# A trunk with two PEER layers on one core: the first tile's x in PSUM, half of a low half on GpSimd, gates in smaller pieces, and another share of the gathers in u

## The chip, the core and the metric

The kernel runs on one core of one Trainium2 chip. The metric is the device time of one execution in microseconds (us). TensorE is PE in the profile, VectorE DVE, ScalarE ACT, GpSimd POOL; SP only issues transfers.

## What is computed

Two layers over 512 tokens of width 1024, each a mixer (chunked gated linear attention in the first, stick-breaking attention in the second, both with memory attention) followed by a PEER retrieval. The change lies in PEER alone:

```python
def peer(x, w_q, subkeys, u_tab, v_tab):
    q = (xf @ w_q).reshape(N, PEER_HEADS, 2, PEER_QHALF)
    s = jnp.einsum('nhpd,hpkd->nhpk', q, subkeys)
    top_s, top_i = lax.top_k(s, PEER_TOPK)
    ...
    idx = jnp.take_along_axis(cand_i, best_pos, axis=-1)
    g = jax.nn.softmax(best_s, axis=-1)
    def apply_experts(args):
        xt, it, gt = args
        act = jax.nn.gelu(jnp.einsum('nd,nhkd->nhk', xt, u_tab[it]), approximate=False)
        return jnp.einsum('nhk,nhkd->nd', gt * act, v_tab[it])
```

There are 16384 experts with a row of 1024 in each of the tables u and v. Each token takes 8 heads x 16 experts.

## The kernel before

Most tokens don't gather. For 352 of the 512 tokens the kernel multiplies x with the whole table u (128 blocks of 128 experts), applies gelu, multiplies with a dense matrix of gates that is zero but for the chosen experts, and multiplies the result with the whole table v (for 384 tokens). Products in fp32 are made of a high and a low half: `split` (L86) lets ScalarE round a block to the high half (uh), and VectorE subtracts it from the block to get the low half (ul). TensorE then makes three products per chunk: 24 matmuls for a block of u.

The first tile of 128 tokens gathers its expert rows instead: `gather` (L1165) is an indirect DMA, issued by GpSimd, of one row for each of the 128 tokens, 512 KB into one of four buffers `gr`. In u a VectorE instruction multiplies gr with the tile's x and sums it (a product); in v one adds gr times a weight to `va`. There are 128 of each, and 32 more gathers in u for the last 32 tokens (the side gathers, with their own x, `xr`). Three gathers are kept ahead (PF).

**Order.** The orders on PE, ACT, DVE and POOL are those in which the code is written (`manual_schedule`); SP's is made by the framework's scheduler. The u stage is a loop of `ublock(b)`, b = 0 to 128. A block does in this order: load block b+2 and make its uh (`prep`; the subtraction that makes ul is only put on a list, `later`); the 24 matmuls into `ph`; gelu of the block before; a step or two of building gates (`gst`: one-hots `ob` on VectorE, scaled ones `obl`, matmuls into `pg`, and from there the gates `gt`, written to DRAM as `Gd`); some selection work (`work`: top-16 of the scores and indices), in which `topk16` may hand the listed subtraction to GpSimd; then `flush` subtracts on VectorE what is still listed; then gather products, as many as `room` gives credit for (`gus`). `room` is a count of VectorE time from constants (BLK, SUM, LOW, HOT, REST), with lowest and highest values GU, GUA, GUX, GUZ, GUM; WB and WB0 are the credit of the selection.

Gates come in 24 groups of 16 tokens (`Gd[sub]`), the last two of them for the side gathers' tokens. Before, all of u uses a PSUM pool of eight banks.

In v a loop runs over 128 blocks, each with `vprep(b + 2)` (load vr, split it into vh and vl, multiply gates with the activations to w, split w), 18 matmuls into six accumulators, and gathers by the credit `vb` (L1844), which spreads what u has left. Gates are loaded by `preload` (L1790): those of a group of 16 blocks (GB) are 24 x 128 x 256 numbers and come in four pieces (GP) in four blocks, from ten blocks (GA) ahead. The first group of six blocks (g0, in a tile named keep) is loaded whole at block 126, where `vprep` begins (BX).

Of the kernel before, what the change touches and what calls it, by code (L numbers as in the profile page):

```python
# [10 lines left out]
F32 = mybir.dt.float32  # L11
# [3 lines left out]
AF = mybir.ActivationFunctionType  # L15
# [59 lines left out]
def psum(E, name="ps", tag="ps"):  # L75
    p, tags = E.ps
    return p.tile([P, 512], F32, tag=tag, name=name, bufs=tags[tag])

# [7 lines left out]
def split(E, raw, name, pool=None, tag="", later=None, eng=None, rows=None):  # L86

    nc = E.nc
    eng = eng or nc.vector
    pool = pool or E.hl  # L90
    if callable(pool):
        hi, lo = pool(f"{name}h"), pool(f"{name}l")
    else:
        hi = pool.tile([P, D], F32R, tag=tag + "hi", name=f"{name}h")
        lo = pool.tile([P, D], F32R, tag=tag + "lo", name=f"{name}l")
    if rows is None:
        nc.scalar.activation(hi, raw, AF.Copy)  # L97
        sub = lambda eng=eng: eng.tensor_sub(lo, raw, hi.bitcast(F32))  # L98
    else:
        nc.scalar.activation(hi, raw, AF.Copy, scale=rows)  # L100
        sub = lambda: eng.scalar_tensor_tensor(lo, raw, rows, hi.bitcast(F32), op0=ALU.mult, op1=ALU.subtract)
    if later is None:
        sub()
    else:
        later.append(sub)
    return hi, lo
# [888 lines left out]
def x_to_T(E, t, tag="ps"):  # L995

    nc = E.nc
    for g in range(2):
        ps = psum(E, name="xtp", tag=tag)
        for j in range(4):  # L1000
# [57 lines left out]
T0 = T - TD  # L1058
KEEP = 16
KB = P - KEEP  # L1060
TS = 16
# [8 lines left out]
GB = 16  # L1070
GA = 10
GP = 4
OT = 4
DT = 8
WB, WB0 = 820, 1600
GU, GUA, GUX, GUZ, GUM = 700, 1500, 1600, 1300, 2400
BG = 118
BLK, SUM, LOW, HOT, REST = 3950, 450, 1150, 1900, 1.12
WP = 1100
# [10 lines left out]
GR = 1.2  # L1090
BX = 126
GR2 = 1.5
# [23 lines left out]
def peer(E, mixer, wq, sk, ut, vt, un, lng, lnb, out_dram=None, follow=()):  # L1116
# [11 lines left out]
    with ExitStack() as pp:  # L1128
# [17 lines left out]
        next(mixer)  # L1146
        pp.enter_context(psum_pool(E, ps=8))
        for _ in mixer:
# [13 lines left out]

        gcount, known = [0], [0]

        def gather(tab, k, idx=None):  # L1165
# [35 lines left out]
        def gather_u():  # L1201
            nu, pend = 0, []

            def issue():
# [6 lines left out]
                if nu < min(P, known[0]):  # L1211
                    pend.append((gh, nu, E.x[:, 0], gather(un, nu)))
                    nu += 1
                    return True
# [6 lines left out]
            while pend:  # L1221
                dst, k, xr, gr = pend.pop(0)
                V.scalar_tensor_tensor(gr, gr, 1.0, xr, op0=ALU.mult, op1=ALU.mult, accum_out=dst[:, k:k + 1])
                if dst is not gh and k == TS - 1:
# [34 lines left out]
        with ExitStack() as up:  # L1259
# [3 lines left out]
            nc.scalar.dma_start(skt, sk)  # L1263
            later = []
            did = dict(low=0, hot=0, sum=0)

            def topk16(*jobs, pool=True):
# [15 lines left out]
                for v, i, s, s2 in jobs:  # L1283
                    nc.vector.max_index(i[:, 8:16], v[:, 8:16], s2)
                return WP if done else 0
# [433 lines left out]
            gst = Stream(gates(list(range(0, S0, OT))), gates(list(range(0, P, OT))), side_gates(0), gates(list(range(0, P, OT))), side_gates(1))  # L1719
            lead.c = -2000.0  # L1720
            ab, ph = None, None
            big = keep = g0 = None

            def ublock(b):
# [26 lines left out]
                else:  # L1751
                    work(WB if ready else WB0)
                flush()
                hot, low, sums = (did[k] - was[k] for k in ("hot", "low", "sum"))
                room = BLK + SUM * sums - HOT * hot - LOW * (1 - low) - REST * (lead.used + work.used - used)
                if b < P - 1:
                    gus(min(max(room, GU), GUA if work.q else GUX if b < BG else GUZ), GUM)
                if LOG:
                    print("block", b, len(work.q), len(gst.q), len(gus.q), gcount)
# [28 lines left out]
        pre = {}  # L1788

        def preload(i):  # L1790

            for c, c1 in zip(gcuts[1:], gcuts[2:]):
                q = i - max(1, c - GA)
                if 0 <= q < GP:
                    if q == 0:
                        pre[c] = new_gates(c, c1)
                    load_gates(pre[c], vorder[c], vorder[c] + c1 - c, slice(q * NSUB // GP, (q + 1) * NSUB // GP))

        def vprep(i):
# [5 lines left out]
            if i in gcuts:  # L1805
                if i == 0:
                    vp["g"] = g0
                    load_gates(g0, b, b + G0)
                else:
                    vp["g"] = pre.pop(i)  # L1810
                vp["i"] = i
# [26 lines left out]
        with written:  # L1838
            for b in range(BX, P + 1):
                ublock(b)  # L1840
                if b < P:
                    vprep(b - BX)
            acc = [[psum(E, name=f"acc{t}_{h}") for h in range(2)] for t in range(ND)]
# [31 lines left out]
            for t in range(ND):  # L1875
# [14 lines left out]
                if last:  # L1890
                    finish(t + 1, parts)
                elif t < ND - 1:
                    if t == 0:
                        E.low.pop(0)()
                    finish(t + 1, parts, (lambda: x_to_T(E, t), lambda: E.low.pop(0)()))
                else:
                    finish(t + 1, parts)
# [87 lines left out]
```

## Time and profile before

| | us |
|---|---|
| median of 3 runs | 2816.67 (2816.49 to 2821.19) |
| profiled execution | 2823.67 |
| its span, first to last instruction | 2821.9 |
| TensorE busy | 2794.7 |
| VectorE busy | 2395.9 |
| ScalarE busy | 1440.5 |
| GpSimd busy | 938.1 |

The stages of the span: the first mixer and the queries of its PEER layer to about 331 us, u to 880, v to 1390, the second mixer and queries to 1736, u to 2284, v to 2790, and the end. A row of a windows view gives, for a stretch, the busy us of each engine with its instructions, the granted clock (1.00 is full), the busy share of the 16 DMA engines and GB/s. A row of a timeline gives start, length, engine, line, operation and, in brackets, how long the engine was idle before it and who ended that. A row of the groups gives busy us and mean ns of one, then idle us before them.

### The profile page before, as it was taken

To read this page: it belongs to the slowest core of one execution; us is meant where nothing else is said; L and a number is where in the kernel's file an instruction comes from. 1 tells how busy PE (TensorE), PEld (TensorE's weight loads), DVE (VectorE), ACT (ScalarE), POOL (GpSimd) and SP (SyncE) were. 2 spreads that over 40 slices of the span, in tenths; PEclk is the share of its full clock that TensorE was granted. 3 is DMA by queue.
4 is the path that set the end of the run, shared out by engine and by line. 5 is a ranking of instruction groups with operands and counts; after the bars stand their busy time and mean duration, and the time that the engine had idled before them with its cause. 6 is when DMAs were issued, how large, how long until landed. Compare 5 with 4: busy or idle time off the path is not lost.

```text
span 2821.9 us, 44857 instructions
## 1 busy us (share of the span) xinstructions
PE 2794.7 (99%) x16235; PEld 2475.7 (88%) x16235; DVE 2395.9 (85%) x4816; ACT 1440.5 (51%) x2699; POOL 938.1 (33%) x665
## 2 busy tenths in 40 slices
PE   9999999999999999999999999999999999999998
PEld 8888899999999888778787889999999988888786
DVE  5565999999876889889968859999998878898888
ACT  6342458576854334334446434585868544344342
POOL 0102433443342344345100024334533433444440
PEclk9999999999999999999999999999999999999999
DMA  5332489999999999999611325899999999999994
GB/s 193 110 112 75 162 294 359 332 354 320 388 338 381 358 373 394 376 373 387 241 68 50 116 83 186 304 355 325 351 325 386 350 366 364 377 393 390 376 389 169
DMA packets 275471, 821.27 MB, mean 291 GB/s; under 512 B 35152, under 2 KB 84528, under 8 KB 268848
## 3 DMA queue, kind: packets, MB, share of 16 engines
q1 hardware_dynamic: 168000, 421.32, 41.8%
q0 software_dynamic: 82944, 302.03, 29.2%
q10 hardware_dynamic: 24304, 95.06, 8.4%
q8 instruction: 127, 2.08, 0.3%
q14 instruction: 96, 0.79, 0.1%
HBM read 723.31 MB, written 92.90 MB: 289 GB/s over the span
## 4 chain that ended last, share of the span: by engine, by line
PE 69%; DVE 11%; issue 9%; DMA 7%; POOL 3%; ACT 1%; ACTq 0%; POOLq 0%; SPq 0%; DVEq 0%
PE acc L289 9%; PE acc L291 9%; PE acc L293 9%; PE ph L117 6%; PE ph L119 6%; PE ph L118 6%; POOL gr L1169 3%; DMA vr<-in_vt 3%; PE pq L117 2%; PE pq L118 2%; PE pq L119 2%; DMA ur<-in_ut 2%; DVE gr L1111 2%; DVE ul L1111 1%; PE bsp L117 1%
## 5 line engine op out<-in xcount | busy, mean ns | idle before, releaser
L117 PE MATMUL ph<-xhl,uh 128*128 128x352 f32 x2048 | 675.0, 330 | 0.2 <-ACT uh L97 0.2
L119 PE MATMUL ph<-xhl,ul 128*128 128x352 f32 x2048 | 662.2, 323 | 2.5 <-DVE ul L1111 2.5
L118 PE MATMUL ph<-xhl,uh 128*128 128x352 f32 x2048 | 661.3, 323 | 0.0
L1169 POOL DMA_INDIRECT gr<-in_un,gidx x256 | 342.1, 1336 | 600.0 <-DVE gr L1111 473.8
L1169 POOL DMA_INDIRECT gr<-in_vt,gidx x256 | 361.7, 1413 | 458.8 <-DVE va L1249 394.8
L289 PE MATMUL acc<-vh,whi 128*128 128x512 f32 x1480 | 457.1, 390 | 5.3 <-ACT whi L1833 5.1
L97 ACT ACTIVATE vh<-vr 128x1024 fp32r<-128x1024 f32 x248 | 262.5, 1059 | 389.9 <-PE acc L293 224.5
L291 PE MATMUL acc<-vl,whi 128*128 128x512 f32 x1480 | 456.8, 390 | 0.6
L293 PE MATMUL acc<-vh,wlo 128*128 128x512 f32 x1480 | 455.8, 389 | 0.0
L97 ACT ACTIVATE uh<-ur 128x1024 fp32r<-128x1024 f32 x288 | 303.6, 1054 | 212.4 <-PE ph L118 145.2
L98 DVE TENSOR_TENSOR vl<-vr,vh 128x1024 fp32r<-128x1024 f32 x248 | 302.9, 1222 | 117.1 <-ACT vh L97 116.8
L119 PEld LDWEIGHTS ph<-xhl,ul 128*128 128x128 f32 x2048 | 385.7, 188 | 4.9 <-DVE ul L1111 4.4
L117 PEld LDWEIGHTS ph<-xhl,uh 128*128 128x128 f32 x2048 | 386.0, 188 | 0.6 <-ACT uh L97 0.5
L118 PEld LDWEIGHTS ph<-xhl,uh 128*128 128x128 f32 x2048 | 386.3, 189 | 0.0
L289 PEld LDWEIGHTS acc<-vh,whi 128*128 128x128 f32 x1480 | 277.0, 188 | 66.5 <-ACT whi L1833 9.9
L291 PEld LDWEIGHTS acc<-vl,whi 128*128 128x128 f32 x1480 | 277.0, 188 | 61.0 <-DVE vl L98 4.0
L1249 DVE SCALAR_TENSOR_TENSOR va<-gr,gw,va 128x1024 f32<-128x1024 f32 x254 | 325.2, 1280 | 4.2 <-DMA gr<-in_vt,gidx 2.1
L293 PEld LDWEIGHTS acc<-vh,wlo 128*128 128x128 f32 x1480 | 277.0, 188 | 58.7 <-DVE wlo L1834 1.9
L1111 DVE SCALAR_TENSOR_TENSOR gr<-gr,xnat 128x1024 f32<-128x1024 f32 x256 | 311.9, 1229 | 19.4 <-DMA gr<-in_un,gidx 19.4
L1111 DVE TENSOR_TENSOR ul<-ur,uh 128x1024 fp32r<-128x1024 f32 x230 | 279.5, 1218 | 28.4 <-ACT uh L97 28.3
L98 POOL TENSOR_TENSOR ul<-ur,uh 128x1024 fp32r<-128x1024 f32 x50 | 120.0, 2401 | 470.2 <-DVE s L1278 330.0
L1593 ACT ACTIVATE obl<-ob,rat 128x128 f16<-128x128 f16 x704 | 224.0, 392 | 49.2 <-DVE ob L1111 32.6
(389 smaller groups left out, 4474.4 us busy)
## 6 DMA issues: line engine op xcount, KB each, us to landing
ur<-in_ut SPq DMA_DIRECT2D x256, 512.0 KB, 6.1
vr<-in_vt SPq DMA_DIRECT2D x256, 512.0 KB, 8.1
Gd<-gt ACTq DMA_DIRECT2D x48, 1024.0 KB, 7.8
gl<-Gd SPq DMA_DIRECT2D x56, 768.0 KB, 14.9
Ad<-act ACTq DMA_DIRECT2D x112, 352.0 KB, 6.2
al<-Ad SPq DMA_DIRECT2D x112, 352.0 KB, 7.3
ur<-in_wq SPq DMA_DIRECT2D x32, 512.0 KB, 3.4
bs<-in_b_st SPq DMA_DIRECT2D x14, 512.0 KB, 3.4
```

The costliest lines, as they stand in the source:

```text
L97: nc.scalar.activation(hi, raw, AF.Copy)
L98: sub = lambda eng=eng: eng.tensor_sub(lo, raw, hi.bitcast(F32))
L117: nc.tensor.matmul(ps, h, xhi[:, c, sl], start=(c == 0), stop=False)
L118: nc.tensor.matmul(ps, h, xlo[:, c, sl], start=False, stop=False)
L119: nc.tensor.matmul(ps, l, xhi[:, c, sl], start=False, stop=(c == NC - 1))
L289: nc.tensor.matmul(acc[hf], lh, hi[:, hf * 512:(hf + 1) * 512], start=first, stop=False)
L291: nc.tensor.matmul(acc[hf], lh, lo[:, hf * 512:(hf + 1) * 512], start=False, stop=False)
L293: nc.tensor.matmul(acc[hf], ll, hi[:, hf * 512:(hf + 1) * 512], start=False, stop=last)
L1111: self.ins = op(*args, **kw)
L1169: nc.gpsimd.indirect_dma_start(out=gr, out_offset=None, in_=tab, in_offset=bass.IndirectOffsetOnAxis(ap=idx[:, k:k + 1], axis=0))
L1249: nc.vector.scalar_tensor_tensor(va, gr, gw[:, k:k + 1], va, op0=ALU.mult, op1=ALU.add)
L1593: nc.scalar.activation(obl[:, q], ob[:, q, 0], AF.Copy, scale=rat[:, n0 + q:n0 + q + 1])
```

## The change

Seven things change.

1. Ahead of block 0 of u the pool of eight banks is closed and one of six banks and a tile of two banks (`xs`) is opened. ScalarE copies the first tile's x there, and the products of its gathers read x from PSUM (named x_3282 in the order below). Side gathers read theirs from SBUF as before. Later `x_to_T` takes the same tile for its transposes.
2. When a gather product of the first tile is due and a subtraction is still listed, VectorE subtracts columns 0 to 511 and GpSimd columns 512 to 1023. GpSimd's part is made to wait for the VectorE instruction just ahead of the two.
3. `flush` now comes after the gathers instead of before them.
4. The credits differ: BLK 4200 for 3950, 550 more where a subtraction is listed, GU 1000 for 700, GUX 1400 for 1600, GUZ 1350 for 1300, WB 850 for 820. By the code's running count of gathers, 152 instead of 141 are issued in each layer by the end of u, and v has 11 fewer. At block 20 the count is 30 instead of 25, at block 82 it is 101 instead of 88, at block 112 136 instead of 125.
5. Gates of the first two groups (6 and 10 blocks) are loaded in four pieces at blocks 119 to 129; those of the third in eight pieces; of all others in twelve pieces, one a block from 14 blocks ahead.
6. The selection's and gates' pools are closed at block 119 (BX) instead of 126; `vprep` still begins at 126 (VB).
7. `topk16` records its last instruction as one that GpSimd can be told to wait for.

```diff
+    if tag == "xs":
+        return p.tile([P, D], F32, tag=tag, name=name, bufs=tags[tag])
...
-        sub = lambda eng=eng: eng.tensor_sub(lo, raw, hi.bitcast(F32))
+        sub = lambda eng=eng, sl=slice(None): eng.tensor_sub(lo[:, sl], raw[:, sl], hi[:, sl].bitcast(F32))
...
+    both = psum(E, name="xtp", tag=tag) if tag == "xs" else None
...
-        ps = psum(E, name="xtp", tag=tag)
+        ps = both[:, g * 512:(g + 1) * 512] if tag == "xs" else psum(E, name="xtp", tag=tag)
...
+LW = 512
+HALF = 550
...
-GA = 10
-GP = 4
+GA = 14
+GE = (-7, -6, -2, 0), (-4, -1, 2, 3), 5
...
-WB, WB0 = 820, 1600
-GU, GUA, GUX, GUZ, GUM = 700, 1500, 1600, 1300, 2400
+WB, WB0 = 850, 1600
+GU, GUA, GUX, GUZ, GUM = 1000, 1500, 1400, 1350, 2400
...
-BLK, SUM, LOW, HOT, REST = 3950, 450, 1150, 1900, 1.12
+BLK, SUM, LOW, HOT, REST = 4200, 450, 1150, 1900, 1.12
...
-BX = 126
+BX = 119
+VB = 126
...
+                if xr is None:
+                    xr = xnat[-1]
+                    if later and len(xnat) > 1:
+                        did["half"] += 1
+                        low, was = later.pop(0), V.ins
+                        low(V, slice(0, LW))
+                        after(E, low(nc.gpsimd, slice(LW, D)), was)
                 V.scalar_tensor_tensor(gr, gr, 1.0, xr, op0=ALU.mult, op1=ALU.mult, accum_out=dst[:, k:k + 1])
...
+            qp.close()
+            pp.enter_context(psum_pool(E, ps=6, xs=1))
+            xnat.append(psum(E, name="x0", tag="xs"))
+            nc.scalar.activation(xnat[1], E.x[:, 0], AF.Copy)
...
-                flush()
                 hot, low, sums = (did[k] - was[k] for k in ("hot", "low", "sum"))
                 room = BLK + SUM * sums - HOT * hot - LOW * (1 - low) - REST * (lead.used + work.used - used)
                 if b < P - 1:
+                    room += HALF * len(later)
                     gus(min(max(room, GU), GUA if work.q else GUX if b < BG else GUZ), GUM)
+                flush()
...
+        for n, c in enumerate(gcuts[:-1]):
+            if n < 2:
+                steps = list(zip(GE[n], ((16, 22), (0, 8), (8, 16), (22, 24))))
+            else:
+                i, w = (GE[2], 3) if n == 2 else (c - GA, 2)
+                steps = [(i + s // w, (s, s + w)) for s in range(0, NSUB, w)]
+            for i, subs in steps:
+                gplan.setdefault(i, []).append((c, slice(*subs)))
```

**VectorE at the second group of side gates.** This is in u of the first layer, after the selection has ended (blocks 106 to 111, near 790 to 816 us). `ob<-iota,iT` and `ob<-ob,gT` are the one-hots of gates, `ob<-iota,siT` and the row behind it those of the side gates, `gr,gh<-gr,xnat` is a gather product. Before:

```order
L1111 TENSOR_TENSOR ob<-iota,iT 128x2048
L1111 TENSOR_TENSOR ob<-ob,gT 128x8x128
L1111 TENSOR_TENSOR ul<-ur,uh 128x1024
L1111 SCALAR_TENSOR_TENSOR gr,gh<-gr,xnat 128x1024 x2
L1111 TENSOR_TENSOR ul<-ur,uh 128x1024
L1111 SCALAR_TENSOR_TENSOR gr,gh<-gr,xnat 128x1024
L1111 TENSOR_TENSOR ul<-ur,uh 128x1024
L1111 SCALAR_TENSOR_TENSOR gr,gh<-gr,xnat 128x1024
L1111 TENSOR_TENSOR ul<-ur,uh 128x1024
L1111 SCALAR_TENSOR_TENSOR gr,gh<-gr,xnat 128x1024 x2
L1111 TENSOR_TENSOR ob<-iota,siT 128x2048
```

Now, at the same place:

```order
L1117 TENSOR_TENSOR ob<-iota,iT 128x2048
L1117 TENSOR_TENSOR ob<-ob,gT 128x8x128
L1117 TENSOR_TENSOR ul<-ur,uh 128x512
L1117 SCALAR_TENSOR_TENSOR gr,gh<-gr,x_3282 128x1024
L1117 TENSOR_TENSOR ul<-ur,uh 128x512
L1117 SCALAR_TENSOR_TENSOR gr,gh<-gr,x_3282 128x1024
L1117 TENSOR_TENSOR ul<-ur,uh 128x512
L1117 SCALAR_TENSOR_TENSOR gr,gh<-gr,x_3282 128x1024
L1117 TENSOR_TENSOR ul<-ur,uh 128x512
L1117 SCALAR_TENSOR_TENSOR gr,gh<-gr,x_3282 128x1024
L1117 TENSOR_TENSOR ob<-iota,siT 128x2048
```

Four products stand between the last one-hots of gates and the first of the side gates instead of six, and each subtraction is half as wide.

**GpSimd in the last third of u.** Before, one row holds the 90 gathers from u's table that follow the last subtraction on GpSimd:

```order
L98 TENSOR_TENSOR ul<-ur,uh 128x1024
L1169 DMA gr<-in_un,gidx 128x1024
L98 TENSOR_TENSOR ul<-ur,uh 128x1024
L1169 DMA gr<-in_un,gidx 128x1024 x2
L98 TENSOR_TENSOR ul<-ur,uh 128x1024
L1169 DMA gr<-in_un,gidx 128x1024 x90
```

Now, at the end of u (the last row reaches into v):

```order
L1178 DMA gr<-in_un,gidx 128x1024
L100 TENSOR_TENSOR ul<-ur,uh 128x512
L1178 DMA gr<-in_un,gidx 128x1024
L100 TENSOR_TENSOR ul<-ur,uh 128x512
L1178 DMA gr<-in_un,gidx 128x1024 x2
L100 TENSOR_TENSOR ul<-ur,uh 128x512
L1178 DMA gr<-in_un,gidx 128x1024
L100 TENSOR_TENSOR ul<-ur,uh 128x512
L1178 DMA gr<-in_un,gidx 128x1024 x10
```

A subtraction of 512 columns now stands between two gathers nearly everywhere.

**SP in v.** The gate pieces of one group of 16 blocks among the loads of v's blocks (`vr`) and of activations (`al`). Before, from the fourth group on:

```order
L1786 DMA gl<-Gd 128x6x256
L82 DMA vr<-in_vt 128x1024
L1786 DMA gl<-Gd 128x6x256
L82 DMA vr<-in_vt 128x1024
L1817 DMA al<-Ad 128x704
L1786 DMA gl<-Gd 128x6x256
L82 DMA vr<-in_vt 128x1024
L1786 DMA gl<-Gd 128x6x256
L82 DMA vr<-in_vt 128x1024
```

Now:

```order
L1806 DMA gl<-Gd 128x2x256 x3
L84 DMA vr<-in_vt 128x1024
L1806 DMA gl<-Gd 128x2x256 x3
L84 DMA vr<-in_vt 128x1024
L1806 DMA gl<-Gd 128x2x256
L1842 DMA al<-Ad 128x704
L1806 DMA gl<-Gd 128x2x256
L84 DMA vr<-in_vt 128x1024
L1806 DMA gl<-Gd 128x2x256 x3
L84 DMA vr<-in_vt 128x1024
L1806 DMA gl<-Gd 128x2x256
```

The twelve pieces stand ahead of five loads of vr instead of four, up to three pieces together.

More of the change, by code (lines that the diff above doesn't have):

```diff
@@ L1146, in peer @@
         next(mixer)
-        pp.enter_context(psum_pool(E, ps=8))
+        qp = ExitStack()
+        qp.enter_context(psum_pool(E, ps=8))
         for _ in mixer:
@@ L1163, in peer @@
         gcount, known = [0], [0]
+        did = {}
+        later, xnat = [], [E.x[:, 0]]
         def gather(tab, k, idx=None):
@@ L1211, in issue @@
                 if nu < min(P, known[0]):
-                    pend.append((gh, nu, E.x[:, 0], gather(un, nu)))
+                    pend.append((gh, nu, None, gather(un, nu)))
                     nu += 1
@@ L1263, in peer @@
             nc.scalar.dma_start(skt, sk)
-            later = []
-            did = dict(low=0, hot=0, sum=0)
+            did.update(low=0, half=0, hot=0, sum=0)
             def topk16(*jobs, pool=True):
@@ L1283, in topk16 @@
                 for v, i, s, s2 in jobs:
-                    nc.vector.max_index(i[:, 8:16], v[:, 8:16], s2)
+                    V.max_index(i[:, 8:16], v[:, 8:16], s2)
                 return WP if done else 0
@@ L1788, in peer @@
         pre = {}
-        def preload(i):
[L1792 to L1797, printed above, removed]
+        gplan = {}
+        for n, c in enumerate(gcuts[:-1]):
[6 more added lines that the diff above has]
+                gplan.setdefault(i, []).append((c, slice(*subs)))
+        def preload(i):
+            for c, subs in gplan.get(i, ()):
+                c1 = gcuts[gcuts.index(c) + 1]
+                if c not in pre:
+                    pre[c] = g0 if c == 0 else new_gates(c, c1)
+                load_gates(pre[c], vorder[c], vorder[c] + c1 - c, subs)
         def vprep(i):
@@ L1805, in vprep @@
             if i in gcuts:
[L1806 to L1810, printed above, removed]
+                vp["g"] = pre.pop(i)
                 vp["i"] = i
@@ L1840, in peer @@
                 ublock(b)
-                if b < P:
-                    vprep(b - BX)
+                if VB <= b < P:
+                    vprep(b - VB)
+                elif b < VB:
+                    preload(b - VB)
             acc = [[psum(E, name=f"acc{t}_{h}") for h in range(2)] for t in range(ND)]
@@ L1894, in peer @@
                         E.low.pop(0)()
-                    finish(t + 1, parts, (lambda: x_to_T(E, t), lambda: E.low.pop(0)()))
+                    finish(t + 1, parts, (lambda: x_to_T(E, t, "xs"), lambda: E.low.pop(0)()))
                 else:
```

## The prediction

> **What bounds the kernel now.** I read the page first, then the stages in windows, then the short windows in which TensorE idles, then its waits. On the page TensorE is busy for 99% of the span. The stage table says where the rest lies; its columns are busy us (and instructions) of PE, PEld, DVE, ACT and POOL, then granted clock, DMA share and GB/s. Rows one to four are the first PEER layer (u with the late selection, u with the last gates, the end of u, v), rows five to eight the second.
>
> ```profile
> span 2821.9 us, 44857 instructions
> ```
>
> ```profile
> core 0: us, PE busy (x) PEld busy (x) DVE busy (x) ACT busy (x) POOL busy (x), PEclk, DMA share, GB/s
> ...
> 410.00:680.00 270.00, 269.13 (x1947) 261.57 (x1946) 264.47 (x660) 197.86 (x418) 111.27 (x74) 1.00 0.95 343
> 680.00:820.00 140.00, 137.17 (x1036) 133.68 (x1035) 120.05 (x167) 101.40 (x230) 56.35 (x39) 0.99 0.97 368
> 820.00:880.00 60.00, 59.78 (x395) 59.10 (x394) 39.01 (x54) 21.21 (x32) 22.07 (x16) 1.00 0.94 320
> 883.00:1390.00 507.00, 503.82 (x2213) 413.87 (x2211) 444.55 (x558) 204.79 (x378) 205.04 (x146) 1.00 0.98 368
> ...
> 1814.00:2084.00 270.00, 268.14 (x1936) 259.75 (x1935) 261.99 (x649) 195.56 (x416) 110.23 (x72) 1.00 0.94 341
> 2084.00:2224.00 140.00, 138.61 (x1054) 135.10 (x1054) 121.44 (x170) 102.89 (x231) 56.00 (x39) 1.00 0.98 367
> 2224.00:2284.00 60.00, 59.15 (x389) 58.17 (x388) 38.48 (x54) 21.22 (x32) 22.93 (x16) 1.00 0.95 335
> 2287.00:2790.00 503.00, 501.70 (x2208) 413.19 (x2206) 443.68 (x556) 205.27 (x377) 200.45 (x146) 1.00 0.99 371
> ```
>
> TensorE's idle time by row is 0.87, 2.83, 0.22, 3.18 and 1.86, 1.39, 0.85, 1.30 us: 12.5 us together. The change leaves TensorE's instructions as they are, so this, and what a pause costs behind it, is all that can be won. VectorE is full (98%) in the first row and has room later; the transfers are near full everywhere. The idle time is in few places:
>
> ```profile
> 800.00:820.00 20.00, 17.17 (x122) 16.65 (x121) 15.91 (x26) 10.62 (x21) 10.84 (x7) 0.91 1.02 400
> 1160.00:1180.00 20.00, 18.41 (x81) 14.54 (x79) 11.70 (x15) 5.96 (x10) 4.99 (x5) 1.00 1.03 388
> 1220.00:1240.00 20.00, 18.53 (x79) 13.89 (x77) 10.79 (x13) 5.83 (x10) 4.64 (x4) 1.00 1.04 392
> ...
> 2200.00:2220.00 20.00, 18.62 (x142) 17.93 (x140) 15.97 (x23) 13.49 (x29) 10.09 (x7) 1.00 1.02 406
> 2260.00:2280.00 20.00, 19.15 (x118) 18.57 (x118) 10.51 (x15) 7.06 (x11) 7.50 (x5) 1.00 1.08 372
> 2620.00:2640.00 20.00, 18.90 (x82) 14.95 (x82) 11.44 (x14) 5.84 (x10) 4.75 (x4) 1.00 1.04 394
> ```
>
> In 800 to 820 us the clock fell to 0.91 as well: 20 x 0.09 = 1.8 us more. The ceiling is 12.5 + 1.8 = **14.3 us**, 0.5%. TensorE's waits name who was late (total, times, longest):
>
> ```profile
> PE acc L289 <- ACT whi L1833: 5.7, 9, 1.5
> PE pg L1547 <- DVE ob L1111: 4.2, 2, 2.8
> PE ph L119 <- DVE ul L1111: 2.5, 4, 1.2
> ```
>
> Row two is one wait in each layer, at the second group of side gates. VectorE's timeline ahead of it:
>
> ```profile
> 809.62 1.23 DVE L1111 SCALAR_TENSOR_TENSOR gr<-gr,xnat 128x1024 f32<-128x1024 f32 x1 [1.68 <-DMA gr<-in_un,gidx]
> ...
> 812.35 1.23 DVE L1111 SCALAR_TENSOR_TENSOR gr<-gr,xnat 128x1024 f32<-128x1024 f32 x1 [1.50 <-DMA gr<-in_un,gidx]
> ...
> 813.50 1.22 DVE L1111 TENSOR_TENSOR ob<-iota,siT 128x2048 bf16<-128x2048 f16 x1
> ```
>
> VectorE works in order. Two products waited 1.68 and 1.50 us for their gathers to land, and the one-hots that TensorE needed stood behind them. The waits of v go back to a weight block that landed late (chain of waits; start, length), 1160 to 1180 us being where gate pieces were in the queue:
>
> ```profile
> 1153.86 18.35 DMA vr<-in_vt
> ```
>
> **The change, part by part.** *Half of a low half on GpSimd.* In the built program each layer has 91 blocks in which VectorE subtracts columns 0 to 511 and GpSimd the rest: 16 before 410 us, 29 in the first row of the table, 33 in the second, 13 in the third.
>
> ```profile
> L97 ACT ACTIVATE uh<-ur 128x1024 fp32r<-128x1024 f32 x288 | 303.6, 1054 | 212.4 <-PE ph L118 145.2
> ...
> L1111 DVE TENSOR_TENSOR ul<-ur,uh 128x1024 fp32r<-128x1024 f32 x230 | 279.5, 1218 | 28.4 <-ACT uh L97 28.3
> ...
> L1834 DVE TENSOR_TENSOR wlo<-w,whi 128x384 fp32r<-128x384 f32 x256 | 141.1, 551 | 0.0
> ...
> L98 POOL TENSOR_TENSOR ul<-ur,uh 128x1024 fp32r<-128x1024 f32 x50 | 120.0, 2401 | 470.2 <-DVE s L1278 330.0
> ```
>
> From 551 ns at 384 columns and 1218 ns at 1024, 512 columns take 551 + 128 x 667/640 = 685 ns on VectorE: 0.53 us saved per half. GpSimd's half takes between 1.2 us (half of 2401 ns) and 2.4 us; I take 1.2, since long rows are nearly linear. That is 91 x 1.2 = 109 us per layer on an engine that the table shows busy for less than half of every row. VectorE saves 48 us per layer.
>
> *x in PSUM.* What GpSimd does to VectorE is in the trace. POOL's subtraction ran from 597.08 to 599.50 us, and the product that met it took 2.08 us; a product with one operand in PSUM (pd) beside it was not touched:
>
> ```profile
> 597.08 2.42 POOL L98 TENSOR_TENSOR ul<-ur,uh 128x1024 fp32r<-128x1024 f32 x1
> ```
>
> ```profile
> 598.51 2.08 DVE L1111 SCALAR_TENSOR_TENSOR gr<-gr,xnat 128x1024 f32<-128x1024 f32 x1
> ```
>
> ```profile
> 137.32 2.55 POOL L98 TENSOR_TENSOR arl<-ar,arh 128x1024 fp32r<-128x1024 f32 x1 [5.30 <-ACT arh L97]
> ```
>
> ```profile
> 137.53 2.64 DVE L599 SCALAR_TENSOR_TENSOR S<-S,dec,pd 128x128 f32<-128x128 f32 x7
> ```
>
> Seven in 2.64 us is the usual pace. So a product from PSUM runs beside GpSimd's half, and where it would have met a whole subtraction it saves the 0.8 us. Its own length: of the 512-column rows below the first reads SBUF alone, the second PSUM (oacc) and SBUF.
>
> ```profile
> L1039 DVE SCALAR_TENSOR_TENSOR xnat<-lny,lnsm,bet 128x512 f32<-128x512 f32 x32 | 22.6, 750 | 0.6
> ...
> L1022 DVE SCALAR_TENSOR_TENSOR lny<-xnat,oacc 128x512 f32<-128x512 f32 x16 | 10.3, 683 | 14.1 <-PE oacc L293 13.9
> ```
>
> PSUM is no slower, so I take 1.22 us as now; the bound above is 2 x 683 = 1.37 us, 0.15 us on each of 128. The copy of x is one ACTIVATE of some 1.05 us per layer ahead of block 0, covered by the two weight blocks that are split ahead; uncovered it is 2 x 1.05 us. The pool of six banks instead of eight still holds two blocks' tiles (a block takes two or three); if ScalarE ran a block late, TensorE would wait up to one uh, 1.05 us, each time. Both at nothing.
>
> The two halves themselves have both operands in SBUF, so by the first two of these rows they go one behind the other. The Trainium skill, SBUF — State Buffer, section "Who interferes with whom", says that a VectorE instruction with two SBUF inputs contends with a GpSimd instruction that reads SBUF, and that issue order decides who blocks. The rows at 597 to 598 us agree (2.08 us where 1.22 is usual). By this rule the change could also lose: see the rivals.
>
> *More gathers in u.* By the kernel's own count 152 instead of 141 are issued by the end of u: 5 more before 410 us, 8 more in row one, 2 fewer in row two, none in row three. In row one VectorE gets 8 x 1.22 = 9.8 us and loses 29 x 0.53 = 15.4: from 264.5 to 259 of 270. In row two 33 x 0.53 and two products go: 120 to 100 of 140. The transfers of row one grow by 8 x 0.524 MB in 270 us, 343 to 359 GB/s, where 20 us windows above reach 406.
>
> *Where gathers are issued.* GpSimd now stands with its half between two gathers. Before, it ran ahead: it waited for the product that frees the buffer and issued at once.
>
> ```profile
> POOL gr L1169 <- DVE gr L1111: 569.4, 190, 18.5
> ```
>
> ```profile
> DMA to landing us min/median/max: 4.2/8.0/13.4
> ```
>
> ```profile
> L1111 DVE SCALAR_TENSOR_TENSOR gr<-gr,xnat 128x1024 f32<-128x1024 f32 x38 | 45.8, 1220 | 6.0 <-DMA gr<-in_un,gidx 6.0
> ```
>
> The last row is of 680 to 820 us: 38 products, one in 3.68 us. Gather n+3 could be issued at the end of product n-1, so it had 4 x 3.68 - 1.22 = 13.5 us, as long as the slowest landing. Now it is issued behind half n, that is about at the end of product n (0.69 + 1.2 against 0.69 + 1.22 us): with 36 products 3 x 3.89 - 1.22 = 10.4 us. The median of 8.0 still fits; the slowest come 3 us late. Behind a late product on VectorE stand the next block's one-hots and half, and TensorE waits for those. But both are made a block or more ahead, and VectorE has 40 us to spare there. Bounds 0 and 12 us (the rival below); I take **+3.0 us** over both layers, near the lower end, as the median fits.
>
> *Side gates.* Before the second group's one-hots VectorE now has four products in four blocks where it had six, so the prefetch is not drained. Of 2.83 + 1.39 + 1.8 = 6.0 us I leave 1.0: **-5.0 us**. *VectorE late in row one and five:* of 0.87 + 1.86 us, half goes with its lighter load: **-1.3**.
>
> *Gate pieces in v.* A group of 16 blocks has 3 MB of gates:
>
> ```profile
> gl<-Gd SPq DMA_DIRECT2D x56, 768.0 KB, 14.9
> ```
>
> ```profile
> L98 DVE TENSOR_TENSOR vl<-vr,vh 128x1024 fp32r<-128x1024 f32 x121 | 147.8, 1222 | 59.6 <-ACT vh L97 59.5
> ...
> L98 DVE TENSOR_TENSOR vtail<-vr,vtail 128x1024 fp32r<-128x1024 f32 x4 | 4.9, 1218 | 0.0
> ```
>
> In 883 to 1390 us stand 125 blocks, 4.06 us each, at 368 GB/s: 1.49 MB a block, 1.30 without gates. Four pieces of 0.79 MB on four blocks make 2.08 MB each, where 392 GB/s carry 1.59: 0.49 x 4 = 2.0 MB behind, 5.0 us. Twelve pieces of 0.26 MB stand by SP's order over five blocks, and eleven gathers fewer take 0.05 MB off each block: 1.88 MB, 0.29 x 5 = 1.45 MB, 3.7 us. The lag shrinks by 1.3 us; the three idle stretches were 1.59, 1.47 and 1.10 us, so 0.3, 0.2 and 0 stay: **-3.6 us**. SP's eight issues more per group lie on a queue that waits anyway. *Gates of the first groups* are loaded before the end of u: of 0.22 + 0.85 us **-0.7**. The loop's start at 119 instead of 126 moves only the second pool; its queues are empty by then.
>
> Sum: -5.0 - 1.3 - 3.6 - 0.7 + 3.0 = **-7.6 us**. The profiled execution took 2823.67 us (span 2821.9), 7.0 above the median 2816.67; the timed runs spread over 4.7 us. Some idle time of the profile may be missing in the median run. Without the stall at 800 to 820 us (4.6 us, of which I let go 3.9) the sum is -3.7. The same place stalls in layer two (2200 to 2220 us), so I take it as usual and nearly all of the sum: -7.2, **2809.5 us**.
>
> **The rivals.** *The waits stay (2815).* SP's order still puts three pieces, 0.79 MB, ahead of a vr, as now; then v keeps its 4 us, and if half of the side gates' 5.0 goes, -2.5 - 1.3 - 0.7 + 3.0 = -1.5 us. For it: five blocks are not many more than four. Against it: fewer gathers everywhere in v.
>
> *All of it goes (2802.5):* the ceiling of 14.3 us.
>
> *Gathers land too late (slower).* Place: u at 680 to 820 and 2084 to 2224 us. It decides from a mean landing of 10.4 us on. At 10.9 every three gathers cost 0.5 us, 12 times in each layer: +12 us, less v's 3.6: 2825. For it: the slowest at 13.4. Against it: the median, and two gathers fewer there.
>
> *GpSimd gets the port first (slower).* If its half starts ahead, VectorE's half waits 1.2 us. In row one the 259 us plus 29 x 1.2 = 35 us times the share of such blocks exceeds 270 from a share of 0.3 on; at one half it is 7 us a layer: +14, less 3.6: 2827. This is what the rule of the Trainium skill on issue order would give. Against it: VectorE's half follows the instruction that GpSimd must first be told of.
>
> **How the numbers follow.** About 0.2% (5.6 us) is what a measurement can tell from no change. Forecast 0.50 (its own range -4 to -12, so 0.38 beyond 0.2% and 0.12 within), waits stay 0.22 (within), all goes 0.12 (faster), late gathers 0.10 and the port 0.06 (slower). That makes faster 0.50, same 0.34, slower 0.16. The range ends at 2801 (the ceiling, and 1.4 us for slow restarts counted as busy) and at 2821, which leaves out the two slower cases.
>
> **What would show it.** PE's waits on DVE ob gone and the clock row at 1.00 near 810 us; the two halves in sequence, GpSimd's seen at 1.2 us or, with the wait, 1.9; the product at 1.22 us beside it; VectorE's waits for gr in 680 to 820 us grown from 6.0 us to 10 or 20; v's idle below 1 us a layer. Wrong would make it: VectorE halves of 1.9 us, products waiting more than 2 us on the average, or v's idle stretches unchanged.

## The result and the profile after

The changed kernel takes **2852.25 us** (median of 4 runs, 2842.57 to 2853.94) where the kernel before took 2818.80 on the same chip (4 runs, 2816.49 to 2821.19). The ratio is 1.0106, with an interval of 1.0092 to 1.0121 (the quotient of the two medians is 1.0119): slower by 1.1%, outside the predicted range of 2801 to 2821 us. The profiled execution took 2853.13 us, 29.5 us more than the one before.

The stage table of the changed kernel (columns as in the table of before; the stretches end later because u takes longer):

```profile
span 2851.4 us, 45518 instructions
```

```profile
410.00:690.00 280.00, 268.96 (x1913) 258.94 (x1912) 259.28 (x666) 197.06 (x417) 156.84 (x109) 0.99 0.93 340
690.00:830.00 140.00, 140.00 (x1063) 136.65 (x1062) 104.78 (x158) 101.83 (x230) 89.76 (x68) 1.00 0.97 367
830.00:889.00 59.00, 59.00 (x393) 58.61 (x392) 35.12 (x60) 21.45 (x33) 43.19 (x34) 1.00 1.02 373
892.00:1400.00 508.00, 506.97 (x2231) 417.69 (x2230) 439.27 (x544) 207.57 (x385) 162.36 (x136) 1.00 0.97 355
1400.00:1440.00 40.00, 33.95 (x182) 29.36 (x182) 26.62 (x47) 6.63 (x13) 1.68 (x6) 0.87 0.17 54
1831.00:2106.00 275.00, 260.89 (x1841) 250.00 (x1840) 248.55 (x639) 190.55 (x407) 148.76 (x104) 0.98 0.92 333
2106.00:2246.00 140.00, 140.00 (x1064) 136.76 (x1064) 110.74 (x174) 103.83 (x232) 90.62 (x69) 1.00 0.97 366
2246.00:2314.00 68.00, 68.00 (x457) 67.48 (x456) 40.09 (x68) 25.97 (x39) 47.40 (x37) 1.00 1.02 380
2318.00:2818.00 500.00, 500.00 (x2208) 414.03 (x2206) 431.78 (x533) 201.47 (x374) 158.50 (x135) 1.00 0.97 357
```

Three of the four stages that were to get better did. The rows of the last gates, of the end of u and of v have hardly any idle time left (0, 0, 1.03 and 0, 0, 0 us). But in row one and in row six (410 to 690 and 1831 to 2106 us) TensorE now idles 11.04 and 14.11 us, where it was 0.87 and 1.86, and the clock is 0.99 and 0.98. And the end of v in the first layer (1400 to 1440 us) has 6 us of idle time and a clock of 0.87. VectorE is busy for 259 us in row one, the number forecast, here in 280 us instead of 270: TensorE waits for an engine that itself has gaps. The waits (total, times, longest) say for what:

```profile
PE ph L121 <- DVE ul L1117: 18.9, 15, 3.6
PE xtp L1005 <- DVE xhl L1010: 6.0, 2, 3.3
PE ph L121 <- POOL ul L100: 5.7, 3, 3.5
PE acc L291 <- ACT whi L1858: 2.0, 6, 0.3
...
DVE gr L1117 <- DMA gr<-in_un,gidx: 71.1, 51, 4.0
...
DVE gr L1117 <- DMA gr<-in_un,si: 7.1, 3, 3.7
```

VectorE's waits for gathers in u grew from 19.7 us (19.4 + 0.3) to 78.2. In 410 to 690 us they grew from 0 to 12.6 us, in 1831 to 2106 us from 0.3 to 15.8. The transfers themselves didn't get slower. From issue to landing a gather now takes

```profile
DMA to landing us min/median/max: 4.4/7.6/12.4
```

where it was 4.2, 8.0 and 13.4 us: they are issued later. One late gather, GpSimd's timeline first, then VectorE's, then TensorE's and its window:

```profile
419.96 1.51 POOL L100 TENSOR_TENSOR ul<-ur,uh 128x512 fp32r<-128x512 f32 x1 [0.83 <-ACT gt L1632]
421.62 1.79 POOL L1178 DMA_INDIRECT gr<-in_un,si  x1 [0.15 <-issue]
```

```profile
427.23 1.22 DVE L1117 SCALAR_TENSOR_TENSOR gr<-gr,xr 128x1024 f32<-128x1024 f32 x1
...
431.63 1.22 DVE L1117 SCALAR_TENSOR_TENSOR gr<-gr,xr 128x1024 f32<-128x1024 f32 x1 [3.18 <-DMA gr<-in_un,si]
...
432.78 1.22 DVE L1117 TENSOR_TENSOR ul<-ur,uh 128x1024 fp32r<-128x1024 f32 x1
```

```profile
430.63 0.32 PE L120 MATMUL ph<-xhl,uh 128*128 128x352 f32 x1
434.05 0.66 PE L121 MATMUL ph<-xhl,ul 128*128 128x352 f32 x1 [3.10 <-DVE ul L1117]
434.51 0.50 PE L119 MATMUL ph<-xhl,uh 128*128 128x352 f32 x1
434.80 0.50 PE L120 MATMUL ph<-xhl,uh 128*128 128x352 f32 x1
...
437.51 0.32 PE L121 MATMUL ph<-xhl,ul 128*128 128x352 f32 x1
```

```profile
434.00:437.00 3.00, 2.95 (x10) 2.95 (x11) 2.97 (x5) 1.11 (x4) 0.81 (x1) 0.50 0.99 379
```

The gather stands behind a half on GpSimd and is issued at 421.62 us. A side product (xr) waits 3.18 us for it and starts as it lands, 10.0 us after the issue; behind it stands a whole subtraction (ul), and TensorE waits 3.10 us for that. Then it pays again: the granted clock is 0.50, and up to 437.2 us its matmuls start 0.29 us apart instead of 0.16. The Trainium skill, TensorE: Matmul & The Clock Gate, Part 1 on the clock gate, says that after an idle window of about 3.4 us the array runs at half rate; the trace agrees in the rate, but here a pause of 3.10 us was enough.

Not every pause is of this kind. Of the 25 us in the two stretches some 14.5 stand within 8 us of a wait for a gather; in the 8 us ahead of the other 10 us VectorE waited for none.

The other loss is at the transposes of the new x at the end of v. After, then before:

```profile
1400.28 0.60 PE L1005 MATMUL xtp<-ident,xnat 128*128 128x128 f32 x4
1404.18 1.12 PE L1005 MATMUL xtp<-ident,xnat 128*128 128x128 f32 x4 [3.30 <-DVE xhl L1010]
...
1418.94 0.66 PE L1005 MATMUL xtp<-ident,xnat 128*128 128x128 f32 x4 [2.75 <-DVE xhl L1010]
```

```profile
1396.00 1.03 PE L1002 MATMUL xtp<-ident,xnat 128*128 128x128 f32 x8
```

Eight transposes in one run have become four, a wait for VectorE's read of the first four, and four more.

### The profile page after: what moved, and what is told of

It is laid out like the page before. It is cut to its first block, busy times and chain, and to the rows that moved or that the text cites. A ratio compares the mean times of both kernels' runs of the same rounds, so it can differ in the third digit from the quotient of the medians.

```text
span 2851.4 us, 45518 instructions
## 1 busy us (share of the span) xinstructions
PE 2805.7 (98%) x16235; PEld 2487.3 (87%) x16235; DVE 2326.3 (82%) x4816; ACT 1441.1 (51%) x2701; POOL 1106.0 (39%) x847
## 4 chain that ended last, share of the span: by engine, by line
PE 85%; DVE 8%; DMA 3%; issue 2%; ACT 1%; POOL 1%; ACTq 0%; DVEq 0%; SPq 0%; POOLq 0%
PE acc L291 12%; PE acc L293 12%; PE acc L295 11%; PE ph L119 9%; PE ph L121 9%; PE ph L120 8%; DMA gr<-in_un,gidx 2%; PE pq L119 2%; PE pq L120 2%; PE pq L121 2%; DVE gr L1117 2%; DVE ul L1117 1%; PE pss L1700 1%; PE pg L1628 1%; DVE ob L1117 1%
## 5 line engine op out<-in xcount | busy, mean ns | idle before, releaser
L121 PE MATMUL ph<-xhl,ul 128*128 128x352 f32 x2048 | 667.0, 326 | 24.6 <-DVE ul L1117 18.9
L100 POOL TENSOR_TENSOR ul<-ur,uh 128x512 fp32r<-128x512 f32 (+1 forms) x232 | 394.9, 1702 | 711.9 <-DVE s L1293 343.6
L1178 POOL DMA_INDIRECT gr<-in_vt,gidx x256 | 306.7, 1198 | 566.9 <-DVE va L1265 511.1
L1117 DVE SCALAR_TENSOR_TENSOR gr<-gr,x 128x1024 f32<-128x1024 f32 x250 | 302.4, 1215 | 71.4 <-DMA gr<-in_un,gidx 71.1
L1178 POOL DMA_INDIRECT gr<-in_un,gidx x256 | 288.1, 1125 | 135.1 <-DVE gr L1117 93.1
L1117 DVE TENSOR_TENSOR ul<-ur,uh 128x512 fp32r<-128x512 f32 (+1 forms) x230 | 184.0, 800 | 40.7 <-ACT uh L99 40.7
```

The costliest lines, as they stand in the source:

```text
L100: sub = lambda eng=eng, sl=slice(None): eng.tensor_sub(lo[:, sl], raw[:, sl], hi[:, sl].bitcast(F32))
L121: nc.tensor.matmul(ps, l, xhi[:, c, sl], start=False, stop=(c == NC - 1))
L1117: self.ins = op(*args, **kw)
L1178: nc.gpsimd.indirect_dma_start(out=gr, out_offset=None, in_=tab, in_offset=bass.IndirectOffsetOnAxis(ap=idx[:, k:k + 1], axis=0))
```

## The experiments

Ten kernels ran. Four names for theories: **Flight** (GpSimd's half stands ahead of the issue of the next gather, so gathers land too late), **Order** (the subtraction stands behind a side product that waits), **Load** (the new credits give VectorE too much in 410 to 690 us), **Tile** (x_to_T has one tile for both halves). The kernel before ran beside them in each of three sets, with medians 2818.65 (first four kernels), 2821.01 (next four) and 2819.58 us (last two); a difference in us between kernels of different sets is good to about 2 us.

The table has the median, the ratio to the kernel before with its interval, and from each profile the length of u (end of its first matmul into ph to end of its last) and of v (from there to the end of the last matmul into acc), for both layers. Each length is from one profile. The changed kernel and the next one have the same code in u, and their lengths of u differ by 3.0 and 3.7 us, so differences of that size in u say nothing; v of the second layer took 524.6 us in five kernels with the same v.

| kernel | us | ratio | u1 | u2 | v1 | v2 |
|---|---|---|---|---|---|---|
| before | 2818.80 | | 551.2 | 550.5 | 531.6 | 527.5 |
| changed | 2852.25 | 1.0106 (1.0092 to 1.0121) | 561.1 | 566.3 | 537.5 | 524.6 |
| transposes first | 2841.41 | 1.0081 (1.0064 to 1.0097) | 564.1 | 562.6 | 526.9 | 524.6 |
| subtraction ahead of side product | 2839.32 | 1.0076 (1.0060 to 1.0093) | 557.3 | 556.6 | 535.9 | 524.6 |
| gather issued ahead of half | 2831.00 | 1.0045 (1.0028 to 1.0062) | 553.8 | 554.0 | 536.0 | 524.6 |
| old credits | 2836.13 | 1.0068 (1.0051 to 1.0085) | 548.4 | 552.1 | 540.3 | 530.2 |
| three repairs | 2817.12 | 0.9988 (0.9978 to 0.9997) | 551.1 | 550.6 | 526.9 | 524.6 |
| three repairs, old credits | 2813.99 | 0.9973 (0.9962 to 0.9985) | 546.2 | 544.8 | 530.9 | 528.4 |
| three repairs, credits between | 2814.25 | 0.9975 (0.9965 to 0.9986) | 549.8 | 550.5 | 526.5 | 524.5 |
| x read from SBUF | 2912.67 | 1.0324 (1.0306 to 1.0341) | 592.8 | 593.6 | 535.7 | 525.1 |
| repairs, old credits, no halves | 2827.43 | 1.0025 (1.0016 to 1.0035) | 552.1 | 555.0 | 529.8 | 529.5 |
| repairs, credits by place | 2804.86 | 0.9947 (0.9932 to 0.9961) | 544.7 | 543.5 | 528.1 | 526.2 |

### All eight transposes ahead of their reads

```diff
-        for j in range(4):
-            c = g * 4 + j
-            nc.tensor.transpose(ps[:, j * P:(j + 1) * P], E.x[:, t, c * P:(c + 1) * P], E.ident)
+    for c in range(8):
+        nc.tensor.transpose(pss[c // 4][:, c % 4 * P:(c % 4 + 1) * P], E.x[:, t, c * P:(c + 1) * P], E.ident)
+    for g in range(2):
+        ps = pss[g]
```

> Theory Tile: at the end of v of the first PEER layer x_to_T writes both halves of its transposes into the one tile xs, so the second four wait for the reads of the first four (waits of 3.30 and 2.75 us, and the clock at 0.81 and 0.91 behind them). With all eight transposes written ahead of the reads both waits go, the clock stays at 1.00 in 1394 to 1435 us, and about 10 us go: near 2842 us against the changed kernel's 2852. Nothing moves in u. Rival: the second four would wait for layer norm or VectorE in any order; then the waits move to another row and the time stays at 2852.

Measured: 2841.41 us, 10.8 less than the changed kernel. The v of the first layer goes from 537.5 to 526.9 us and u does not gain (1126.7 us in both layers together against 1127.4). The windows view over the end of v, in stretches of this kernel:

```profile
1399.00:1414.00 15.00, 14.13 (x67) 10.38 (x66) 13.99 (x24) 6.57 (x11) 0.00 (x0) 1.00 0.51 172
1414.00:1440.00 26.00, 25.99 (x186) 24.17 (x185) 18.70 (x33) 7.69 (x13) 1.87 (x6) 1.00 0.09 31
```

The clock is 1.00 and the wait gone. Tile is right, and its price is 10.6 us: two waits of together 6.05 us, the rest slow matmuls behind them (in the changed kernel the clock is 0.50 from 1404 to 1410 us and 0.66 from 1419 to 1423).

### The subtraction ahead of a side product

```diff
                         after(E, low(nc.gpsimd, slice(LW, D)), was)
+                else:
+                    while later:
+                        later.pop(0)(V)
```

> Only the place of the listed subtraction changes: ahead of a side product instead of behind it. Theory Order: a side product that waits for its gather holds up the subtraction behind it, and TensorE waits for that; then TensorE's idle time in u between 410-690 and 1831-2106 us, 11.0 + 14.1 us, falls below 8 us together and the time to about 2833 us. Theory Flight: gathers simply land too late for any product; then VectorE still waits some 70 us for gr, the first tile's late products and what follows them stay late, and the time falls by 5 us at most. Theory Load: VectorE has too much to do in these stretches; then nothing changes.

Measured: 2839.32 us, 12.9 less. TensorE's waits on VectorE's ul fall from 18.9 to 4.1 us, while VectorE's own waits for gathers stay (71.1 and 68.1 us):

```profile
PE ph L121 <- POOL ul L100: 6.9, 5, 3.4
...
PE ph L121 <- DVE ul L1117: 4.1, 6, 0.9
...
DVE gr L1117 <- DMA gr<-in_un,gidx: 68.1, 50, 3.6
```

Idle time in the two stretches falls to 6.9 and 7.6 us and not below 8 together. So Order carries a part only: behind a product that is late, GpSimd's next half and then the matmuls are still late.

### The gather issued ahead of GpSimd's half

```diff
                 dst, k, xr, gr = pend.pop(0)
+                sent = issue()
...
-                while not issue() and nu < P:
+                while not sent and not issue() and nu < P:
```

> Gather n+3 is issued before GpSimd's half of the block instead of behind it. Theory Flight: the half costs each gather an interval between products, so the prefetch is some 3.9 us shorter; then VectorE's waits for gr fall from 71 us to about 20 to 30 us, as before the change, TensorE's idle time in the two u stretches from 25 us to below 8, and the time to about 2833 us. Theory Order: waits for gr get shorter, but a side product that waits still holds the subtraction behind it; half of the idle time stays, 2843 us. Theory Load: nothing changes.

Measured: 2831.00 us, 21.3 less, the most of any single repair. VectorE's waits for gathers all but vanish, below those of before:

```profile
PE ph L121 <- DVE ul L1117: 10.6, 12, 1.2
...
DVE gr L1117 <- DMA gr<-in_un,gidx: 6.3, 9, 1.4
DVE gr L1117 <- DMA gr<-in_un,si: 1.1, 2, 0.7
```

Flight is right about the waits. It is wrong that they are all: 12.6 us of idle time stay in the two stretches, in 14 pauses of 0.4 to 1.2 us. Ahead of 11 of them VectorE is busy for 4.7 us or more of the last 5, which points to Load and Order.

### The credits of before

The edit puts back BLK 3950, GU 700, GUX 1600, GUZ 1300 and WB 820, and adds nothing for a listed subtraction.

> The credits of before (BLK 3950, nothing more for a listed subtraction, GU 700, GUX 1600, GUZ 1300, WB 820), all else as changed. Theory Load: more products in 410 to 690 us make VectorE late; then TensorE's idle time there falls from 25 us to about 3 us and the time to about 2830 us, and v, which gets more gathers, gains a few us back. Theories Order and Flight: the interval between products grows by some 10 per cent at most, so gathers have a little longer; idle falls by a third at most, the time to 2845 us or stays.

Measured: 2836.13 us, 16.1 less. Idle time in 410 to 690 us falls to 1.07 and in 1831 to 2106 to 0.15 us, although over all of u VectorE waits for gathers as long as with the new credits (81.0 us with the side products):

```profile
PE acc L291 <- ACT whi L1858: 7.4, 9, 3.5
...
PE pg L1562 <- DVE ob L1117: 5.7, 2, 4.1
...
PE ph L121 <- DVE ul L1117: 1.2, 2, 1.1
...
DVE gr L1117 <- DMA gr<-in_un,gidx: 78.2, 52, 4.9
```

In the two stretches themselves these waits are about half of what they were, 7.9 and 6.2 us instead of 12.6 and 15.8, and 23 us of them in each layer fall into the stage of the last gates, where TensorE loses 1.7 and 4.1 us. So late gathers harm TensorE most where VectorE has no room to catch up, and the eight more products took that room: Load and Flight strengthen each other. By the table this run takes 26.9 us off u in both layers, more than the early issue (19.6) or the order (13.5), and v gives 8.4 back for its 11 gathers more. The run shows the other side of the credits too: the wait on the side gates' one-hots (ob) is back, and so are v's waits for whi (7.4 us). In the changed kernel the first was gone and the second 2.0 us, because of the credits.

### The three repairs together, with three sets of credits

> The three repairs together (all eight transposes ahead of the reads, the listed subtraction ahead of a side product, gather n+3 issued ahead of GpSimd's half), the changed kernel's credits kept. The single runs took off 11, 13 and 21 us of 2852. Theory Flight plus Order plus Tile: what is left in u is VectorE working without a pause in some blocks of 410 to 690 us; TensorE's idle there falls from 25 to about 6 to 8 us, and the time to about 2816 us (the effects of order and flight overlap). If the three simply added, 2807 us. Theory Load: the credits alone explain u, then 2828 us or more is left.

> The three repairs and the credits of before (141 gathers by the end of u instead of 152). Theory Load on top of Flight: with fewer products in 410 to 690 us and early issue nothing in u is late any more: idle in u below 2 us in each layer, the side gates' wait on ob (5.7 us in the run with the old credits alone) gone, and the time near 2808 us. v gets the 11 gathers back: if the gates' smaller pieces are what made v faster, its waits for whi stay near 2 us; if it was the fewer gathers, they are at 6 to 7 us as before. If Flight alone explains u, this run is no faster than the three repairs with the new credits.

The credits between are BLK 3950, GU 700, GUX 1500, GUZ 1400, WB 820, HALF 550.

> The three repairs and credits between (BLK 3950, GU 700, GUX 1500, GUZ 1400, WB 820, 550 more for a listed subtraction): 148 gathers by the end of u. Theory Load: idle in 410 to 690 us lies between the two runs beside it, 2 to 4 us a layer, v between too; the time near 2810 us. If v's gathers cost more than u's load, this is the fastest of the three.

Measured: 2817.12, 2813.99 and 2814.25 us. The three repairs alone bring the changed kernel back to just below the kernel before: 35.1 us less than 2852.25, where the single runs add up to 45.0, so Flight and Order overlap by some 10 us. With the new credits 4.19 us stay idle in 410 to 690 us; with the old ones none:

```profile
410.00:690.00 280.00, 275.81 (x1983) 265.82 (x1982) 264.13 (x678) 201.24 (x425) 162.14 (x114) 1.00 0.96 354
```

```profile
410.00:690.00 280.00, 280.00 (x2034) 273.22 (x2033) 259.77 (x669) 204.43 (x429) 147.03 (x102) 1.00 0.94 345
```

The first row is of the new credits, the second of the old ones: VectorE is busy for 264 us in the one and 260 in the other. But the mean load doesn't decide. With the credits between VectorE is busy for 259 us, and 4.13 us stay idle:

```profile
410.00:690.00 280.00, 275.87 (x1991) 267.26 (x1991) 259.31 (x665) 201.08 (x423) 154.45 (x109) 1.00 0.95 346
```

What is left with the new credits and with those between is a few single waits, the longest (2.0 us) for a subtraction that the selection gave to GpSimd whole. What goes with the idle time is the rate in the middle of u: by the traces 47 and 46 gathers are issued between blocks 20 and 60 in these two kernels, 41 with the old credits. The table's v columns answer the question about v. With 152 gathers done by the end of u, v takes 526.9 and 524.6 us; with 141 it takes 530.9 and 528.4, close to before, although its gates come in the same small pieces. The expectation of 2808 us was missed because v gives back 7.8 us. The credits between gain in v what they lose in u.

### x from SBUF

```diff
-            xnat.append(psum(E, name="x0", tag="xs"))
-            nc.scalar.activation(xnat[1], E.x[:, 0], AF.Copy)
+            xnat.append(E.x[:, 0])
```

> The changed kernel, but the products read the first tile's x from SBUF as before, while GpSimd still takes half of the subtractions. If x in PSUM keeps GpSimd's half off the product: products that meet a half take up to 2 us instead of 1.21, their mean rises to 1.5 us or more, GpSimd's half ends later than 1.2 us after its start, and the time rises to 2865 us or more. If the place of x does not matter: 2852 us, the same mean.

Measured: 2912.67 us, 60 us slower than the changed kernel, more than expected. Groups of 410 to 690 us, changed kernel first:

```profile
L1117 DVE SCALAR_TENSOR_TENSOR gr<-gr,x 128x1024 f32<-128x1024 f32 x40 | 48.3, 1214 | 9.3 <-DMA gr<-in_un,gidx 9.2
...
L1117 DVE TENSOR_TENSOR ul<-ur,uh 128x512 fp32r<-128x512 f32 x29 | 19.8, 683 | 0.3 <-ACT uh L99 0.3
...
L100 POOL TENSOR_TENSOR ul<-ur,uh 128x512 fp32r<-128x512 f32 x29 | 43.3, 1493 | 50.5 <-DVE ob L1117 7.7 <-ACT gt L1632 7.6 <-DVE af L1117 7.4
```

```profile
L1117 DVE SCALAR_TENSOR_TENSOR gr<-gr,xnat 128x1024 f32<-128x1024 f32 x36 | 71.7, 2000 | 1.3 <-DMA gr<-in_un,gidx 1.3
...
L100 POOL TENSOR_TENSOR ul<-ur,uh 128x512 fp32r<-128x512 f32 x25 | 37.7, 1506 | 48.0 <-DVE af L1117 12.3 <-DVE ob L1117 7.0 <-ACT uh L99 7.0
```

A product takes 1214 ns with x in PSUM and on the average 2000 ns with x in SBUF. The 2000 ns are a mixture. With x in SBUF a product without a half beside it takes about 1.2 us, and one that meets a half 2.31 us, as it ends about one product's time after the half:

```profile
700.51 1.21 DVE L1117 SCALAR_TENSOR_TENSOR gr<-gr,xnat 128x1024 f32<-128x1024 f32 x1
...
710.80 2.31 DVE L1117 SCALAR_TENSOR_TENSOR gr<-gr,xnat 128x1024 f32<-128x1024 f32 x1
```

```profile
710.52 1.51 POOL L100 TENSOR_TENSOR ul<-ur,uh 128x512 fp32r<-128x512 f32 x1 [4.73 <-DVE i L1117]
```

GpSimd's half does end later than 1.2 us after its start, as expected, but no later than with x in PSUM (1506 and 1493 ns): the product alone pays. The Trainium skill, SBUF — State Buffer, section "Who interferes with whom", says that a VectorE instruction with at most one SBUF input does not contend with GpSimd and one with two does; these rows agree.

### No halves

The three repairs and the old credits, and every subtraction that the selection does not give to GpSimd whole is VectorE's.

> The three repairs with the credits of before, and GpSimd takes no half (its whole subtractions beside the selection stay; x stays in PSUM). If the halves carry u: VectorE in 410 to 690 us goes from 260 us to about 260 + 28 x 0.53 = 275 of 280 us, TensorE waits for ul there, u gets 3 to 6 us longer in each layer and the time is 2820 to 2826 us. If they carry nothing there, because VectorE was not late without them (before the change TensorE lost 0.87 and 1.86 us in these stretches): u as long as with the halves, 545 to 546 us, and the time stays at 2814 us.

Measured: 2827.43 us, ratio 1.0025, against 0.9973 with the halves. VectorE has 270 us to do in 410 to 690 us instead of 260, and TensorE waits again, for ul and for the side gates' one-hots:

```profile
410.00:690.00 280.00, 277.31 (x2008) 269.69 (x2007) 270.16 (x665) 203.19 (x427) 117.08 (x75) 1.00 0.94 343
```

```profile
PE ph L121 <- DVE ul L1117: 8.4, 10, 2.4
...
PE pg L1566 <- DVE ob L1117: 4.9, 2, 3.0
```

The time is 2827 us, a little above the 2820 to 2826 expected. So the half on GpSimd, the heart of the change, is worth 5.9 and 10.2 us of u in the two layers, with x in PSUM and these credits.

### Credits by place

The three repairs, the changed kernel's credits up to block 21, those of before behind it, with GUX and GUZ at 1450: by the code's running count 30 gathers at block 20, 72 at block 60, 144 at the end.

> The three repairs; the changed kernel's credits up to block 21 of u, those of before behind it, and GUX and GUZ at 1450: 30 gathers by block 20, 72 by block 60, 144 by the end of u. Theory Load: blocks 20 to 60 keep the lower load (42 gathers, as before), so u stays at 545 to 546 us a layer; three gathers fewer in v take 1 to 2 us off v, and fewer products ahead of the second side gates shorten the wait on ob (2.5 us) to below 1: near 2809 us, faster than both kernels. If the total issued by block 60 counts and not the rate, u falls back to about 549 us and the time to 2814 us or more.

Measured: **2804.86 us** (5 runs, 2803.94 to 2807.80), ratio 0.9947 (0.9932 to 0.9961): faster than both kernels, and 4 us below the expectation.

```profile
410.00:690.00 280.00, 279.81 (x2026) 272.39 (x2024) 260.29 (x671) 203.59 (x427) 153.33 (x106) 1.00 0.95 347
690.00:830.00 140.00, 140.00 (x1070) 136.61 (x1070) 102.55 (x153) 100.78 (x228) 89.10 (x66) 1.00 0.96 362
```

The rate in blocks 20 to 60 counts, 42 gathers as before the change, and not the total by block 60 (72 against 67). v takes 528.1 and 526.2 us, between the kernels with 141 and 152 gathers in u. No wait on ob or ul is left among TensorE's waits.

## Why the prediction was wrong, step by step

**The step on where gathers are issued** named the right mechanism, saw it in one place only and so priced it too low. It put +3.0 us (bounds 0 to 12) on 680 to 820 us and its twin, because gathers come closest there, and noted that VectorE has 40 us to spare in that stage. Just so: VectorE's waits for gathers in 690 to 830 us are 12.4 us (6.0 before), and TensorE lost nothing there. The same delay applies wherever a half stands ahead of an issue, and in 410 to 690 us VectorE had 20 us in 280 to spare and far less in places: in the 20 us up to the pause of 1.20 us at 493 us it was busy for 19.8. The sum also took products to be evenly spaced, which gave a gather 10.4 us. In the place shown above one product ends at 428.4 us and the next wants its gather at once, 6.8 us after the issue. Undoing this step alone gives 21.3 us back.

**The step "VectorE late in row one and five, -1.3 us"** went by the mean load of the stage, 264 to 259 of 270 us. The mean came out (259.28 us), the conclusion did not: where 1.3 us less idle time was forecast, there are 10.2 and 12.3 us more in the two rows. The gain from halves is spread over the blocks in which a first tile's product is due; a block in which a side product comes first gets none, and there VectorE has a whole subtraction beside the product. Old credits alone give 16.1 us, the subtraction ahead of the side product alone 12.9. The third item of the change, flush behind the gathers, was given no price: the prediction spoke of the next block's half behind a late product and took it to be made a block ahead. TensorE waited for a subtraction up to 3.6 us at a time.

**"Both at nothing", the step on x in PSUM,** weighed the copy and the six banks, rightly as far as the trace shows (TensorE has no idle time in 331 to 410 us and no wait for uh), and left out the last sentence of the change's first item: that x_to_T takes the same tile. One tile for two halves is a wait in each of two x_to_T, 10.6 us.

**Right:** the side gates. Idle time at 690 to 830 and 2106 to 2246 us is 0 and the clock 1.00; that it comes from fewer products ahead of the one-hots is shown by the old credits, with which the wait returns (5.7 us, and 2.5 us where gathers are issued early as well, so late gathers are part of the 5.7). VectorE's half at 685 ns (683 measured), and the product at 1.22 us (1.21). The end of u has no idle time either; that the gate pieces did this is not shown, as with the old credits and the same pieces 0.2 and 0.4 us are back in the first layer. GpSimd's half takes 1.49 us; the 1.2 us taken for it and the 1.9 us named for it with its wait lie on both sides. It takes 1.30 us on the average where VectorE has no subtraction or one-hots beside it and 1.54 where it has.

**Right with the wrong size and reason:** v. The sum had -3.6 us, from smaller pieces and a little from fewer gathers. Where x_to_T is repaired v takes 4.7 and 2.9 us less than before, 7.6 together. Of that only a sliver is the pieces': with 141 gathers and small pieces v stands at 530.9 and 528.4 us, 0.7 below and 0.9 above before. It is the 11 gathers fewer.

Of the rivals none named this outcome. "GpSimd gets the port first" needed VectorE halves of 1.9 us; they took 683 ns, and 681 with x in SBUF. What GpSimd's half delays with x in SBUF is the product behind VectorE's half, 1.1 us each time; x in PSUM kept that away. "Gathers land too late" had the mechanism and the wrong place. How much of the changed kernel's loss in u belongs to each of Flight, Order and Load cannot be said as a sum: undoing each alone takes 13.5 (Order), 19.6 (Flight) and 26.9 us (Load) off u, where the changed kernel lost 25.7, so what they remove overlaps.

## What to carry to other kernels

Work handed to an idle engine also stands in that engine's queue: look for what is issued behind it (here the prefetch), and price the delay in the stage with the least slack, not where the transfers are tightest. An engine's mean load over a stage says little when some blocks get none of the relief; look at the fullest blocks. When a tile is shared or merged, follow every user of it, also the one that comes 1000 us later.

## What the runs showed of the hardware

With x in SBUF VectorE's product beside GpSimd's half grew from 1.21 to 2.31 us while GpSimd's 1.49 us stayed at 1.51. In these rows the instruction that starts second pays: the product behind the half, and the half behind VectorE's subtraction or one-hots (1.54 us on the average where it meets one, 1.30 where it doesn't). x in PSUM shields the product alone: of the changed kernel's 16 one-hots in 690 to 830 us (`ob<-iota,iT`, both operands in SBUF) four took 2.1 to 2.2 us beside a half, where 1.22 is usual. And a pause of 3.10 us of TensorE cost about another 1.2 us: nine times 0.29 us between the starts of matmuls behind it, where 0.16 is usual.
